# Expert weights of a mixture-of-experts decoder layer, loaded in 8 KB runs over permuted rows

## The chip, the cores and the metric

One core of a Trainium2 chip runs one decoder layer over 512 tokens of width 1024, in float32. The metric is device time in microseconds. The kernel before took 638.92 us, the median of 3 runs (637.88 to 639.37).

## What is computed

The layer is a mixer (gated linear attention and a gated convolution), then a hierarchical mixture of 16 experts, then a gated per-layer embedding and a last norm. The change touches the experts alone:

```
for e in range(N_EXPERTS):                      # 16; a token has 2 experts of its best group
    hid = silu(t @ w_gate[e]) * (t @ w_up[e])   # w_gate, w_up: 1024 x 512
    y = y + combine[:, e:e + 1] * (hid @ w_down[e])   # w_down: 512 x 1024
```

`t` is the normed residual stream. The order in which the rows of a weight matrix are summed over is free, as long as the columns of `t` or `hid` come in the same order.

## The kernel before

**Experts.** The normed tokens lie in DRAM as `h2d`, the residual stream as `xd`. For each expert, POOL gathers up to 96 tokens into `xe` (96 partitions x 1024, line 1056, in turn into two buffers, the gather for expert e+4 at the end of iteration e of the loop at line 1245, so a whole expert and more before its use). TensorE transposes them in eight blocks of 128 columns (`transposed`, line 1070, called by `x_tr`, line 1123, once for each half of the columns, four transposes each); ACT and DVE split each transposed block into two fp32r parts, `xT…h` and `xT…l`. `pu` and `pg` (96 x 512) are the products with w_up and w_gate, 24 matmuls each: 8 row blocks of the weights times 3 products of high and low parts (`mm3`, line 1094). silu(pg) * pu is `sg`; `h_tr` (line 1143) transposes it in four blocks to `hT`. `pd` is the product with w_down, in two column halves of 512, each 4 row blocks times 3 products, one half after the other (`stream_mm`, line 1101). ACT evicts each half with the tokens' weights to `ye` (lines 1264 and 1267), and POOL adds the rows of `ye` to `xd` in DRAM by a scatter (`scatter`, line 1112). In iteration e the order on TensorE is pu[e], pg[e+1], pd[e].

**The weights' stream.** `Stream` (line 54) holds a list of loads (`specs`) and a ring of slots of 128 partitions x 8 KB: 13 of them in the expert phase, two of which hold `prjs` (the product of the per-layer embeddings). Each load fills one slot with 1,024 KB. For gate and up it takes 512 rows of 512 columns, for down all 512 rows of 512 of the 1024 columns; row k*128 + p goes to partition p, so that a partition gets four runs of 2 KB (lines 94 to 98). A slot is taken apart in two halves: ACT casts a half (128 x 1024) to the tile `hi` (line 112), DVE computes the rest `lo` (line 113). A half is one `take()`: two row blocks of 512 columns, 6 matmuls. `pump()` starts the next half whenever fewer than `cap` are open (6, in the last four experts 5; `CAPS`). When its second half is done a slot goes back (`give`) and SP issues the next load of the list; `REST` holds back two freed slots in experts 8 to 11 and six from expert 12 on. The loads stand in the order in which TensorE needs them: up[e], gate[e+1], down[e], six for each expert (lines 742 to 750).

**Before and after the experts.** Ahead of expert 0, SP stores `xs` to `xd` and POOL gathers `xe` for experts 0 and 1 (line 1078) while SP issues three loads of experts; then a branch on the fullest expert's count (`overflow`, line 1146, line 1149) is passed; its body runs only where an expert has more than 96 tokens. After expert 14's scatter, SP reads `xd` back (`read_x`, line 1232) and loads w_ple_gate. Expert 15 is added by a matmul (line 1225) instead of a scatter.

Of the kernel before, what the change touches and what calls it, by code (L numbers as in the profile page):

```python
# [13 lines left out]
AF = mybir.ActivationFunctionType  # L14
# [4 lines left out]
P = 128  # L19
# [9 lines left out]
NE = 16  # L29
# [6 lines left out]
CAP = 96  # L36
CH = 2112
HALF = 512
# [14 lines left out]
class Stream:  # L53
# [11 lines left out]
    def add(self, src, r0, nk, c0, cn, c1=None, c1n=0, gain=None):  # L65
        self.specs.append((src, r0, nk, c0, cn, c1, c1n, gain))

    def slot(self, cols, dt=F32):

        at = self.free.pop(0)  # L70
        return at, at[0].tile([P, cols], dt, tag=at[1], name=at[1])
# [11 lines left out]
    def load(self, n=99, parts=1, eng=None):  # L83
        eng = eng or self.nc.sync
        while n and self.free and self.specs:
            n -= 1
            spec = self.specs.pop(0)
            if callable(spec):
                spec()
                continue  # L90
            src, r0, nk, c0, cn, c1, c1n, gain = spec
            w = cn + c1n
            at, raw = self.slot(nk * w)
            v = raw.rearrange("p (k c) -> p k c", k=nk)
            rows = src[r0:r0 + nk * P, :].rearrange("(k p) c -> p k c", p=P)
            for i in range(parts):
                ks = slice(nk // parts * i, nk // parts * (i + 1))
                eng.dma_start(v[:, ks, :cn], rows[:, ks, c0:c0 + cn])
                if c1n:
                    eng.dma_start(v[:, ks, cn:], rows[:, ks, c1:c1 + c1n])  # L100
            self.loaded += [(raw, nk // 2, w, 0, None, gain), (raw, nk // 2, w, 1, at, gain)]

    def split(self, hi=None, lo=None, eng=None, later=False):
        eng = eng or self.nc.vector
# [47 lines left out]
def hymba_layer(ctx, tc, x, p, g_mix, w_in, w_gla_gate, b_gla_gate, g_gla_out, w_conv, w_out,  # L152
# [4 lines left out]
    p, w_in, w_out = p[0, 0], w_in[0], w_out[0]  # L157
    ve, se, pe, ge, sy = nc.vector, nc.scalar, nc.tensor, nc.gpsimd, nc.sync
# [15 lines left out]
    def mm_ps(name):  # L174
        return ps.tile([P, HALF], F32, tag="mm", name=name)
# [4 lines left out]
    def half(i):  # L180
        return slice(i * HALF, (i + 1) * HALF)

    def tok(t):
        return slice(t * P, (t + 1) * P)


    W = Stream(nc, hlp, 6)

    def add_columns(src, c0, c1=None, c1n=0, gain=None):
        for i in range(2):  # L190
            W.add(src, HALF * i, 4, c0, HALF, c1, c1n, gain if gain is None else gain[:, 4 * i:4 * i + 4])
# [7 lines left out]
    ident = consts.tile([P, P], F32, name="ident")  # L199
# [515 lines left out]
    sgs = []  # L715
# [23 lines left out]

    W.specs += [lambda: read_p(), lambda: keep(pTt, F32R)]  # L740
    W.add(w_ple_proj[0], 0, 2, 0, D)
    add_columns(w_exp_gate[0, 0], 0)
    for e in range(NE):
        add_columns(w_exp_up[0, e], 0)
        if e == 0:
            W.specs += [lambda: keep(prjs, F32), lambda: keep(prjs, F32)]
        if e + 1 < NE:
            add_columns(w_exp_gate[0, e + 1], 0)
        for ci in range(2):
            W.add(w_exp_down[0, e], 0, 4, HALF * ci, HALF)  # L750
    sy.dma_start(xd[S:], x[:P])
    merged(proj_steps([f"pC{i}" for i in range(4)], c_out), gla[:12])
    merged(proj_steps([f"pu{i}" for i in range(4)], u_out), gla[12:])
# [150 lines left out]
    sw = rtp.tile([CAP, NE], F32, name="sw", bufs=1)  # L904
# [67 lines left out]
    for k in range(NK):  # L972
        if k % 2 == 0:
            wo.extend(W.take())
        wh, wl = wo[k]
# [9 lines left out]
    for t in range(NT):  # L985
        at = {1: lambda: (square0(t), x1_tr(t, 0))}
# [56 lines left out]
    ye = [mo.tile([P, D], F32, name=f"ye{i}") for i in range(2)]  # L1043
# [23 lines left out]
        return [(hh[:, k * n:(k + 1) * n], hl[:, k * n:(k + 1) * n]) for k in range(4)]  # L1067


    def transposed(src, name, n=CAP):  # L1070

        pt = aux_ps("pt_" + name)
        for k in range(4):
            pe.transpose(pt[:, k * n:(k + 1) * n], src[:n, tok(k)], ident[:n, :n])  # L1074
        return split_T(pt, name, n)

    for e in range(2):
# [16 lines left out]
    def mm3(dst, xT, ws, k0, nk):  # L1094
        for i, (wh, wl) in enumerate(ws):
            k = k0 + i
            xh, xl = xT[k]
            for n, (a, b_) in enumerate(((xh, wh), (xh, wl), (xl, wh))):
                pe.matmul(dst, a, b_, start=(k + n == 0), stop=(k == nk - 1 and n == 2))  # L1099

    def stream_mm(dst, xT, nk, then=(), ahead=True):

        then = dict(then)
        for h in range(nk // 2):
            mm3(dst, xT, W.take(), 2 * h, nk)
            W.done()
            if h in then:
                then[h]()
            if ahead:
                W.pump()  # L1110
# [6 lines left out]
    xTs, hTs, sgs, pgs, pus = {0: xT}, {}, {}, {}, {}  # L1117
# [5 lines left out]
    def x_tr(e, i):  # L1123
        if e < NE:
            xTs.setdefault(e, []).extend(transposed(xe[e % 2][:, half(i)], f"xT{e}_{i}"))
# [5 lines left out]
    def slots_mm(e):  # L1131
        if e < NE and e not in done:
            done.add(e)
            slots(e, oh[e], vals, toki, rowi, sw, f"{e}")

    def rows_of(e):
        if e < NE:
            gather(xe[e % 2][:CAP], col(toki, e))
# [2 lines left out]
        ve.tensor_mul(sgs[e][:CAP], sgs[e][:CAP], pus[e][:CAP])  # L1141

    def h_tr(e):
        hTs[e] = transposed(sgs[e], f"hT{e}")

    def overflow(free_x):

# [57 lines left out]
    def last_one_hot_tr():  # L1205
        pt = aux_ps("pt_ohl")
        for t in range(NT):
            pe.transpose(pt[:CAP, tok(t)], ohl[0][:, t * CAP:(t + 1) * CAP], ident)
        se.copy(ohT, pt[:CAP])
        a0, a1 = Af[:, :, NG - 1, EPG - 1], sec[:, :, NE - 1]  # L1210
        c0 = rt.tile([P, NT], F32, name="cwl0")
        ve.tensor_mul(c0, cw[0], a0)
        ve.tensor_mul(cwl, cw[1], a1)
        ve.tensor_add(cwl, cwl, c0)
# [30 lines left out]
    for e in range(NE - 1):  # L1245
        W.rest, W.cap = REST[e], CAPS[e]
        pus[e] = mm_ps(f"pu{e}")
        if e == 0:
            then = {0: lambda: (slots_mm(2), rows_of(2), slots_oh(3)), 1: lambda: x_tr(1, 0), 2: lambda: x_tr(1, 1),
                    3: lambda: (times_up(0), slots_mm(3), rows_of(3), slots_oh(4))}  # L1250
        else:
            then = {3: lambda: (times_up(e), slots_oh(e + 4))}
        stream_mm(pus[e][:CAP], xTs[e], NK, then)
        pgs[e + 1] = mm_ps(f"pg{e + 1}")
        then = {1: lambda: h_tr(e), 3: lambda: silu(e + 1)}
        if e == NE - 2:
            then[3] = lambda: (silu(e + 1), se.preload_act_table_set("sigmoid_and_others"))
        stream_mm(pgs[e + 1][:CAP], xTs[e + 1], NK, then)
        for ci in range(2):
            pd = mm_ps(f"pd{e}_{ci}")  # L1260
            y_ = ye[e % 2][:CAP, half(ci)]
            if ci == 0:
                first = last_one_hot if e == NE - 4 else lambda: slots_mm(e + 4)
                then = {0: first, 1: lambda: se.activation(y_, pd[:CAP], AF.Copy, scale=sw[:, e:e + 1])}
            else:
                then = {0: lambda: (x_tr(e + 2, 0), last_one_hot_tr() if e == NE - 4 else None),
                        1: lambda: (se.activation(y_, pd[:CAP], AF.Copy, scale=sw[:, e:e + 1]), x_tr(e + 2, 1), rows_of(e + 4))}  # L1267
            stream_mm(pd[:CAP], hTs[e], 4, then, ahead=(e < NE - 2 or ci == 0))
        scatter(ye[e % 2][:CAP], col(rowi, e))


    e = NE - 1
# [103 lines left out]
    for t in range(NT):  # L1376
        n = t + 1
# [78 lines left out]
```

## Time and profile before

| what | value |
|---|---|
| time, median of 3 runs | 638.92 us (637.88 to 639.37) |
| time of the profiled execution | 639.44 us |
| its span, first to last instruction | 637.7 us |
| mean granted TensorE clock | 0.982 of full speed |
| busy: TensorE, its weight loads, DVE, ACT, POOL | 94%, 72%, 75%, 57%, 19% of the span |
| read from and written to HBM | 137.56 MB, 12.71 MB |

The profile is of one execution. Its span leaves out 1.7 us at the two ends. An engine's busy share is a mean over stages: up to about 200 us the projections and the attention run, up to 260 us the output projection and the routing, up to about 575 us the experts, and then the gate of the embeddings. In the rows, L98 and so on are the lines of the kernel before; `raw` and `x` are slots of the stream, `xe`, `ye`, `pu`, `pg`, `pd`, `sg`, `hT` and `xT` the tiles named above, with buffer numbers left out.

### The profile page before, as it was taken

The page shows a single profiled execution, that of the slowest core. Times are in us where ns is not written, and L with a number is a line of the kernel's source. Part 1 is how long each engine was busy: PE and PEld are TensorE (multiplying, and loading weights), DVE is VectorE, ACT ScalarE, POOL GpSimd, SP SyncE. Part 2 cuts the span into 40 slices and gives each one's busy share as a digit, 9 for nine tenths or more (in the row PEclk, how much of TensorE's full clock was granted, in tenths as well). Part 3 has the DMA queues.
Part 4 walks back from the last instruction along what each step waited for, and adds up shares of the span by engine and source line. Part 5 has one row for each costly group of instructions (what it writes and reads, how often), then busy time and mean ns, then how long its engine had stood idle before and what let it go on. Part 6 is the DMA issues. An engine that isn't in the chain of part 4 may idle for free.

```text
span 637.7 us, 8404 instructions
## 1 busy us (share of the span) xinstructions
PE 601.3 (94%) x3006; PEld 457.7 (72%) x3006; DVE 478.1 (75%) x808; ACT 364.8 (57%) x516; POOL 119.9 (19%) x148
## 2 busy tenths in 40 slices
PE   7999989999999999559999999999999999988995
PEld 7987767877787787447777777777777767656784
DVE  4642897852496376457999999999999989888864
ACT  5433626203625233345788877778878878876332
POOL 1530842000240001103222211122222201100011
PEclk9999979999999999889999999999999999999999
DMA  8721211221034957884999999999999999987001
GB/s 270 236 68 67 99 67 66 67 67 66 1 132 154 389 163 286 294 304 150 333 369 368 367 352 353 355 347 348 350 367 360 357 340 361 370 261 277 33 34 66
DMA packets 73007, 148.45 MB, mean 233 GB/s; under 512 B 4797, under 2 KB 5396, under 8 KB 72942
## 3 DMA queue, kind: packets, MB, share of 16 engines
q1 hardware_dynamic: 69054, 136.69, 60.0%
q0 software_dynamic: 3744, 10.89, 7.6%
q8 instruction: 26, 0.43, 0.3%
q10 hardware_dynamic: 160, 0.27, 0.1%
q14 instruction: 23, 0.19, 0.1%
HBM read 137.56 MB, written 12.71 MB: 236 GB/s over the span
## 4 chain that ended last, share of the span: by engine, by line
PE 37%; DMA 9%; DVE 4%; ACT 3%; issue 2%; POOLq 0%; DVEq 0%; ACTq 0%
PE pu L1099 10%; PE pd L1099 10%; PE pg L1099 9%; DMA raw<-in_w_exp_down_dram 6%; PE pgate L1099 5%; DVE lo L113 2%; DMA x<-in_w_exp_down_dram 2%; ACT hi L112 2%; DMA x<-in_w_exp_up_dram 2%; PE pt_xT L1074 1%; PE pgate_last L1409 1%; DVE lo L118 1%; PE pt_hT L1074 1%; PE px L1306 1%; PE pz L1225 0%
## 5 line engine op out<-in xcount | busy, mean ns | idle before, releaser
L113 DVE TENSOR_TENSOR lo<-raw,hi 128x1024 fp32r<-128x1024 f32 x172 | 204.1, 1218 | 21.7 <-ACT hi L112 20.4
L112 ACT CAST hi<-raw 128x1024 fp32r<-128x1024 f32 x172 | 171.8, 1049 | 9.6 <-DMA raw<-in_w_exp_down_dram 8.2
L1056 POOL DMA_INDIRECT xe<-h2d,toki x16 | 28.1, 1759 | 199.9 <-PE pt_xT L1074 160.4
L118 DVE SCALAR_TENSOR_TENSOR lo<-raw,cst,hi 128x512 fp32r<-128x512 f32 (+1 forms) x52 | 41.4, 839 | 18.6 <-ACT hi L117 18.5
L113 DVE TENSOR_TENSOR lo<-x,hi 128x1024 fp32r<-128x1024 f32 x30 | 36.3, 1219 | 5.5 <-ACT hi L112 5.4
L1113 POOL DMA_INDIRECT xd<-ye,rowi x15 | 29.6, 1973 | 51.6 <-ACT ye L1267 47.9
L117 ACT ACTIVATE hi<-raw,cst 128x512 fp32r<-128x512 f32 (+1 forms) x52 | 34.0, 714 | 0.1
L112 ACT CAST hi<-x 128x1024 fp32r<-128x1024 f32 x30 | 30.9, 1050 | 1.7 <-DMA x<-in_w_exp_down_dram 1.4
L1099 PE MATMUL pg<-hi,xT_1h 128*96 128x512 f32 x60 | 24.5, 408 | 0.0
L1099 PE MATMUL pu<-hi,xT_0h 128*96 128x512 f32 x60 | 24.4, 407 | 0.0
L1099 PE MATMUL pu<-lo,xT_1h 128*96 128x512 f32 x60 | 23.8, 396 | 0.0
L1099 PE MATMUL pg<-hi,xT_1l 128*96 128x512 f32 x60 | 23.8, 396 | 0.0
L1099 PE MATMUL pu<-hi,xT_0l 128*96 128x512 f32 x60 | 23.8, 396 | 0.0
L1099 PE MATMUL pu<-hi,xT_1l 128*96 128x512 f32 x60 | 23.8, 396 | 0.0
L1099 PE MATMUL pg<-hi,xT_0h 128*96 128x512 f32 x60 | 23.7, 395 | 0.0
L1099 PE MATMUL pg<-lo,xT_1h 128*96 128x512 f32 x60 | 23.7, 395 | 0.0
L1099 PE MATMUL pg<-lo,xT_0h 128*96 128x512 f32 x60 | 23.7, 395 | 0.0
L1099 PE MATMUL pu<-lo,xT_0h 128*96 128x512 f32 x60 | 23.7, 395 | 0.0
L1099 PE MATMUL pg<-hi,xT_0l 128*96 128x512 f32 x60 | 23.7, 394 | 0.0
L1099 PE MATMUL pu<-hi,xT_1h 128*96 128x512 f32 x60 | 23.6, 394 | 0.0
L632 ACT ACTIVATE sq<-xs 128x512 f32<-128x512 f32 x4 | 2.5, 632 | 35.0 <-DVE xs L614 35.0
L724 POOL TENSOR_TENSOR xs<-xs,sg 128x128 f32<-128x128 f32 x16 | 11.3, 736 | 57.9 <-ACT sg L719 57.9
(539 smaller groups left out, 1591.1 us busy)
## 6 DMA issues: line engine op xcount, KB each, us to landing
raw<-in_w_exp_gate_dram SPq DMA_DIRECT2D x30, 1024.0 KB, 14.4
raw<-in_w_exp_down_dram SPq DMA_DIRECT2D x26, 1024.0 KB, 12.5
raw<-in_w_exp_up_dram SPq DMA_DIRECT2D x25, 1024.0 KB, 15.6
raw<-in_w_in_dram SPq DMA_DIRECT2D x10, 1024.0 KB, 5.1
x<-in_w_exp_up_dram SPq DMA_DIRECT2D x7, 1024.0 KB, 9.6
x<-in_w_exp_down_dram SPq DMA_DIRECT2D x6, 1024.0 KB, 17.5
xs<-in_x_dram SPq DMA_DIRECT2D x16, 256.0 KB, 5.5
raw<-in_w_out_dram SPq DMA_DIRECT2D x4, 1024.0 KB
```

The source lines that it names most:

```text
L112: self.nc.scalar.copy(hi, rw)
L113: los.append(lambda: eng.tensor_sub(lo, rw, hi.bitcast(F32)))
L117: self.nc.scalar.activation(hi[:, c_], rw[:, c_], AF.Copy, scale=g_)
L118: los.append(lambda c_=c_, g_=g_: eng.scalar_tensor_tensor(lo[:, c_], rw[:, c_], g_, hi[:, c_].bitcast(F32), op0=OP.mult, op1=OP.subtract))
L632: se.activation(osq[c], to[c], AF.Square)
L724: ge.tensor_tensor(tv, tv, sgs[i][:, tok(t)], op=OP.mult)
L1056: ge.indirect_dma_start(out=x_, out_offset=None, in_=h2d, in_offset=bass.IndirectOffsetOnAxis(ap=idx, axis=0), bounds_check=S - 1, oob_is_ ...
L1074: pe.transpose(pt[:, k * n:(k + 1) * n], src[:n, tok(k)], ident[:n, :n])
L1099: pe.matmul(dst, a, b_, start=(k + n == 0), stop=(k == nk - 1 and n == 2))
L1113: ge.indirect_dma_start(out=xd, out_offset=bass.IndirectOffsetOnAxis(ap=idx, axis=0), in_=y_, in_offset=None, bounds_check=S + P - 1, oob_ ...
L1306: pe.transpose(pt[:, tok(k)], X(t)[:, ci * HALF + k * P:ci * HALF + (k + 1) * P], ident)
L1409: pe.matmul(pgl[i][:, :256], a, b_[:, 256 * i:256 * i + 256], start=(k + n == 0), stop=(k == NK - 1 and n == 2))
```

## The change

`add_rows` adds a load of whole rows: of a block of nk*128 rows, partition p gets the nk consecutive rows p*nk to p*nk + nk - 1, one run of 8 KB in DRAM and in the slot. For gate and up nk is 4 (512 rows of 2 KB), for down nk is 2 (256 rows of 4 KB, all 1024 columns). Row block k of a slot is then every nk-th row instead of 128 consecutive ones. `transposed` follows: it reads the columns of `xe` with a step of 4 floats, those of `sg` with a step of 2. A half of a slot of down is now one row block of 1024 columns instead of two of 512, so both column halves, `pd[0]` and `pd[1]`, are summed side by side, and both are evicted after the last row block. Expert 15's down keeps the old form.

```diff
+    def add_rows(self, src, r0, nk):
+        self.specs.append((src, r0, nk, None, src.shape[-1], None, 0, None))
...
             at, raw = self.slot(nk * w)
+            self.loaded += [(raw, nk // 2, w, 0, None, gain), (raw, nk // 2, w, 1, at, gain)]
+            if c0 is None:
+                eng.dma_start(raw, src[r0:r0 + nk * P, :].rearrange("(p k) c -> p (k c)", k=nk))
+                continue
...
-    add_columns(w_exp_gate[0, 0], 0)
+    def add_expert(w):
+        for i in range(2):
+            W.add_rows(w, HALF * i, 4)
+
+    add_expert(w_exp_gate[0, 0])
     for e in range(NE):
-        add_columns(w_exp_up[0, e], 0)
+        add_expert(w_exp_up[0, e])
...
-        for ci in range(2):
-            W.add(w_exp_down[0, e], 0, 4, HALF * ci, HALF)
+        for i in range(2):
+            if e + 1 < NE:
+                W.add_rows(w_exp_down[0, e], 2 * P * i, 2)
+            else:
+                W.add(w_exp_down[0, e], 0, 4, HALF * i, HALF)
...
-    def transposed(src, name, n=CAP):
+    def transposed(src, name, n=CAP, nk=4):
         pt = aux_ps("pt_" + name)
         for k in range(4):
-            pe.transpose(pt[:, k * n:(k + 1) * n], src[:n, tok(k)], ident[:n, :n])
+            b_ = (k // nk) * nk * P
+            pe.transpose(pt[:, k * n:(k + 1) * n],
+                         src[:n, b_:b_ + nk * P].rearrange("n (p k) -> n k p", k=nk)[:, k % nk], ident[:n, :n])
...
     def h_tr(e):
-        hTs[e] = transposed(sgs[e], f"hT{e}")
+        hTs[e] = transposed(sgs[e], f"hT{e}", nk=2 if e + 1 < NE else 1)
...
-        for ci in range(2):
-            pd = mm_ps(f"pd{e}_{ci}")
-            y_ = ye[e % 2][:CAP, half(ci)]
...
-            stream_mm(pd[:CAP], hTs[e], 4, then, ahead=(e < NE - 2 or ci == 0))
+        pd = [mm_ps(f"pd{e}_{ci}") for ci in range(2)]
+        def y_out():
+            for ci in range(2):
+                se.activation(ye[e % 2][:CAP, half(ci)], pd[ci][:CAP], AF.Copy, scale=sw[:, e:e + 1])
+        then = {0: last_one_hot if e == NE - 4 else lambda: slots_mm(e + 4),
+                1: lambda: x_tr(e + 2, 0),
+                2: last_one_hot_tr if e == NE - 4 else nop,
+                3: lambda: (y_out(), x_tr(e + 2, 1), rows_of(e + 4))}
+        for k in range(4):
+            (wh, wl), = W.take()
+            for ci in range(2):
+                mm3(pd[ci][:CAP], [None] * k + [hTs[e][k]], [(wh[:, half(ci)], wl[:, half(ci)])], k, 4)
+            W.done()
+            then[k]()
+            if e < NE - 2 or k < 2:
+                W.pump()
```

On ACT, the rows around expert 14's down; ye is the eviction, hi the casts of the stream, hT the transposed sg. Before:

```order
L112 CAST hi<-x_5632 128x1024
L112 CAST hi<-raw_5674 128x1024
L1264 ACTIVATE ye_2307<-pd_0_5780,sw 96x512
L112 CAST hi<-raw_5674 128x1024
L1267 ACTIVATE ye_2307<-pd_1_5802,sw 96x512
L112 CAST hi<-raw_5700 128x1024 x2
```

and with the change:

```order
L120 CAST hi<-x_5641 128x1024
L120 CAST hi<-raw_5674 128x1024 x2
L1281 ACTIVATE ye_2307<-pd_0_5780,sw 96x512
L1281 ACTIVATE ye_2307<-pd_1_5781,sw 96x512
L120 CAST hi<-raw_5700 128x1024 x2
```

The eviction of pd_0 has moved behind the second cast of the slot, next to that of pd_1; the casts are the same.

On TensorE, the middle of expert 13's down with the first transposes of expert 15's xe. Before:

```order
L1099 MATMUL pd_0_5610<-hi,hT13h 96x512
L1099 MATMUL pd_0_5610<-lo,hT13h 96x512
L1099 MATMUL pd_0_5610<-hi,hT13l 96x512
L1099 MATMUL pd_1_5634<-hi,hT13h 96x512
L1099 MATMUL pd_1_5634<-lo,hT13h 96x512
L1099 MATMUL pd_1_5634<-hi,hT13l 96x512
L1099 MATMUL pd_1_5634<-hi,hT13h 96x512
L1099 MATMUL pd_1_5634<-lo,hT13h 96x512
L1099 MATMUL pd_1_5634<-hi,hT13l 96x512
L1074 MATMUL pt_xT_0_5641<-ident,xe_2306 128x96 x4
L1099 MATMUL pd_1_5634<-hi,hT13h 96x512
```

and with the change:

```order
L1117 MATMUL pd_0_5610<-hi,hT13h 96x512
L1117 MATMUL pd_0_5610<-lo,hT13h 96x512
L1117 MATMUL pd_0_5610<-hi,hT13l 96x512
L1117 MATMUL pd_1_5611<-hi,hT13h 96x512
L1117 MATMUL pd_1_5611<-lo,hT13h 96x512
L1117 MATMUL pd_1_5611<-hi,hT13l 96x512
L1091 MATMUL pt_xT_0_5628<-ident,xe_2306 128x96 x4
L1117 MATMUL pd_0_5610<-hi,hT13h 96x512
L1117 MATMUL pd_0_5610<-lo,hT13h 96x512
L1117 MATMUL pd_0_5610<-hi,hT13l 96x512
```

The two halves alternate, three matmuls each for a row block, and the transposes come after the second row block instead of after three quarters of the matmuls. The order of SP's loads and of POOL's instructions is the same as before.

## Rows read from the trace of the kernel before

**Rows 1.** The head of the page: the span, and busy time, share of the span and instructions of each engine; from its part on DMA, the queue on which SP issues the weights' loads, with its packets, MB and the share of 16 engines' time that they took.

```profile
span 637.7 us, 8404 instructions
...
PE 601.3 (94%) x3006; PEld 457.7 (72%) x3006; DVE 478.1 (75%) x808; ACT 364.8 (57%) x516; POOL 119.9 (19%) x148
...
q1 hardware_dynamic: 69054, 136.69, 60.0%
```

**Rows 2.** The table by stretches: the stretch (us from the span's start) and its length, then busy us and instructions of TensorE, its weight loads, DVE, ACT and POOL; then TensorE's granted clock, the DMA engines' share and GB/s. From 214 to 219 us only loads with 2 KB runs are under way; from 256 to 259 us the stores of xs to xd, and from 571 to 573 us the reads of xd, whose runs are 4 KB.

```profile
214.00:219.00 5.00, 5.00 (x25) 4.11 (x24) 2.76 (x4) 2.10 (x4) 0.00 (x0) 1.00 1.04 386
256.00:259.00 3.00, 2.57 (x25) 1.98 (x24) 2.41 (x17) 1.55 (x3) 0.00 (x0) 1.00 1.03 408
262.00:268.50 6.50, 0.28 (x2) 0.00 (x0) 0.51 (x1) 2.30 (x4) 0.22 (x1) 0.81 1.02 334
280.00:290.00 10.00, 3.27 (x13) 2.21 (x12) 2.53 (x9) 2.37 (x3) 0.00 (x0) 0.66 0.80 283
300.00:519.00 219.00, 219.00 (x1072) 155.32 (x1071) 204.03 (x288) 176.40 (x218) 45.40 (x25) 1.00 1.05 353
571.00:573.00 2.00, 2.00 (x10) 1.42 (x9) 2.00 (x3) 2.00 (x4) 0.00 (x0) 1.00 1.01 403
```

**Rows 3.** The chain of work that ended last, in order of time: start us, us, and what.

```profile
282.70 4.11 issue
...
323.39 0.33 PE pt_xT L1074 x4
...
325.45 5.59 PE pu L1099 x24
...
343.43 5.59 PE pu L1099 x24
...
500.13 17.63 DMA raw<-in_w_exp_down_dram
...
542.33 11.34 DMA x<-in_w_exp_down_dram
...
601.99 0.44 PE px L1306 x4
```

**Rows 4.** What TensorE waited for from 300 to 576 us: the engine, line and tile, whom it waited for, us in total, times, longest us.

```profile
PE pd L1099 <- DVE lo L113: 1.5, 3, 0.8
```

**Rows 5.** The timeline of TensorE: start us, us, engine, line, operation, out<-in, shape and count; in brackets the idle time before it and what ended it.

```profile
268.52 0.90 PE L1074 MATMUL pt_xT0a<-ident,xe 96*128 96x96 f32 x4 [6.24 <-DMA xe<-h2d,toki]
...
286.81 0.74 PE L1099 MATMUL pu<-hi,xT0ah 128*96 128x512 f32 x1 [6.73 <-issue]
...
519.28 0.40 PE L1099 MATMUL pd<-hi,hT12h 128*96 128x512 f32 x1
520.20 0.48 PE L1099 MATMUL pd<-lo,hT12h 128*96 128x512 f32 x1 [0.52 <-DVE lo L113]
...
557.70 0.47 PE L1099 MATMUL pd<-hi,hT14h 128*96 128x512 f32 x1
558.96 0.47 PE L1099 MATMUL pd<-lo,hT14h 128*96 128x512 f32 x1 [0.79 <-DVE lo L113]
```

**Rows 6.** What ACT waited for from 290 to 570 us; columns as in rows 4.

```profile
ACT hi L112 <- DMA raw<-in_w_exp_down_dram: 8.2, 6, 2.4
...
ACT hi L112 <- DMA x<-in_w_exp_down_dram: 1.4, 1, 1.4
```

**Rows 7.** The timeline of POOL, which issues the gathers (xe<-h2d) and scatters (xd<-ye); columns as in rows 5.

```profile
259.10 1.86 POOL L1056 DMA_INDIRECT xe<-h2d,toki  x1 [5.57 <-DVE cmaxi L931]
...
561.36 1.41 POOL L1113 DMA_INDIRECT xd<-ye,rowi  x1 [16.17 <-ACT ye L1267]
```

**Rows 8.** The timeline of SP's queue, which issues the loads; columns as in rows 5.

```profile
259.97 0.38 SPq L98 DMA_DIRECT2D raw<-in_w_exp_up_dram  x1
260.46 0.44 SPq L98 DMA_DIRECT2D x<-in_w_exp_up_dram  x1
261.01 0.45 SPq L98 DMA_DIRECT2D x<-in_w_exp_gate_dram  x1
...
569.01 0.82 SPq L1232 DMA_DIRECT2D raw<-xd  x2
```

**Rows 9.** All gathers, line 1056: the time from issue to landing.

```profile
DMA to landing us min/median/max: 5.2/8.1/9.4
```

**Rows 10.** The instructions on the tile pt_xT, the transposed xe: line, engine and operation, count, duration in ns (smallest, median, largest), first and last start, shapes.

```profile
L1074 PEld LDWEIGHTS pt_xT<-ident,xe x120: 137/138/143, 291.1 to 541.8; 96*128 96x128 f32 x120
L1074 PE MATMUL pt_xT<-ident,xe x120: 243/245/247, 291.3 to 541.9; 96*128 96x96 f32 x120
```

**Rows 11.** TensorE's weight loads by line and shape: count, busy us, mean ns, and the idle time before. The operand after the comma is the loaded one, partitions x columns.

```profile
L1099 PEld LDWEIGHTS pg<-lo,xT_1h 128*96 128x96 f32 x60 | 9.8, 163 | 3.2
...
L1225 PEld LDWEIGHTS pz<-raw,ohT 96*128 96x128 f32 x16 | 3.0, 188 | 0.8 <-DVE raw L1220 0.2
```

**Rows 12.** DVE's level products of the decayed keys (line 540); columns as in rows 10.

```profile
L540 DVE TENSOR_TENSOR xs<-F,qkT x28: 407/422/953, 74.5 to 116.8; 64x256 f32<-64x256 f32 x28
```

**Rows 13.** The timelines of ACT and of DVE around expert 14's eviction and the read of xd; columns as in rows 5.

```profile
560.40 0.69 ACT L1267 ACTIVATE ye<-pd,sw 96x512 f32<-96x512 f32 x1 [0.28 <-PE pd L1099]
...
574.94 0.75 DVE L1227 SCALAR_TENSOR_TENSOR raw<-pz,cwl,raw 128x512 f32<-128x512 f32 x1 [0.59 <-PE pz L1225]
```

**Rows 14.** The DMA issues: out<-in, engine, operation, count, KB each, median us from issue to landing.

```profile
raw<-xd SPq DMA_DIRECT2D x4, 512.0 KB, 4.4
```

More of the change, by code (lines that the diff above doesn't have):

```diff
@@ L100, in load @@
                     eng.dma_start(v[:, ks, cn:], rows[:, ks, c1:c1 + c1n])
-            self.loaded += [(raw, nk // 2, w, 0, None, gain), (raw, nk // 2, w, 1, at, gain)]
     def split(self, hi=None, lo=None, eng=None, later=False):
@@ L747, in hymba_layer @@
         if e + 1 < NE:
-            add_columns(w_exp_gate[0, e + 1], 0)
-        for ci in range(2):
-            W.add(w_exp_down[0, e], 0, 4, HALF * ci, HALF)
+            add_expert(w_exp_gate[0, e + 1])
+        for i in range(2):
[3 more added lines that the diff above has]
+                W.add(w_exp_down[0, e], 0, 4, HALF * i, HALF)
     sy.dma_start(xd[S:], x[:P])
@@ L1258, in hymba_layer @@
         stream_mm(pgs[e + 1][:CAP], xTs[e + 1], NK, then)
-        for ci in range(2):
-            pd = mm_ps(f"pd{e}_{ci}")
-            y_ = ye[e % 2][:CAP, half(ci)]
[L1262 to L1267, printed above, removed]
-            stream_mm(pd[:CAP], hTs[e], 4, then, ahead=(e < NE - 2 or ci == 0))
+        pd = [mm_ps(f"pd{e}_{ci}") for ci in range(2)]
[14 more added lines that the diff above has]
+                W.pump()
         scatter(ye[e % 2][:CAP], col(rowi, e))
```

## The prediction

> **What bounds the kernel now.** I read the page's head first: TensorE is busy for 601.3 of 637.7 us, and queue q1, which carries the weights, takes 60% of the DMA engines' time [rows 1]. So two things may bound it, and the share alone does not say which one does where. The second view is the table by stretches. From 300 to 519 us, twelve of the sixteen experts, TensorE is busy for 219.00 of 219.00 us, and the DMA share is 1.05 in the same rows [rows 2]. An expert takes 17.98 us there, the distance of two starts of pu [rows 3]. A faster DMA can therefore give nothing in this stretch: no TensorE time is idle to be taken back.
>
> The same rows show that the DMA is nevertheless short. An expert needs six loads of 1,024 KB, 6.29 MB, and 96 rows of 4 KB gathered and as many scattered, 0.39 MB each: 7.07 MB in 17.98 us, or 393 GB/s, while 353 GB/s arrive [rows 2, 3]. The difference, 0.7 MB an expert, comes out of the weights that already lie in the 11 slots left to the experts (two of the 13 hold prjs). After twelve experts that is 8.6 MB of 11.5, and from expert 8 on two of the slots, from 12 on six are held back as well. This is where the next views fit: the waits of TensorE between 300 and 576 us hold 1.5 us on DVE's lo parts of the weights, three times [rows 4]. The two that matter are at 519.28 and 557.70 us: the next matmul starts 0.92 and 1.26 us later, where 24 of them take 5.59 us, 0.23 us each [rows 3, 5]: 0.69 + 1.03 = **1.72 us lost**. Behind them is a load: ACT's casts waited for in_w_exp_down, and the chain shows 17.63 and 11.34 us between issue and landing [rows 3, 6]. 1.72 us is all that TensorE loses to weights in the expert phase, so it is the upper end of what faster loads can give there.
>
> Ahead of the expert phase are two other idle stretches in which the DMA plays a part. TensorE starts expert 0's transposes at 268.52 us after 6.24 us of waiting for the gather xe, issued at 259.10 us; three expert loads were issued between 259.97 and 261.01 us [rows 5, 7, 8]. And it idles 6.73 us up to 286.81 us, of which 4.11 us stand in the chain as issue, behind the branch on the fullest expert, with q1 at work (share 0.80, 283 GB/s) [rows 2, 3, 5].
>
> **The change, part by part.**
>
> *The loads.* 94 of the 96 expert loads get 8 KB runs instead of 2 KB; number, bytes, order and slots stay. 2 KB runs alone move 386 GB/s (214 to 219 us), transfers in 4 KB runs 403 to 408 GB/s (571 to 573 and 256 to 259 us), 4 to 6% more [rows 2]. No row has 8 KB runs into SBUF; I bound them by no gain and by twice the step from 2 to 4 KB, and take 5%, the middle of the rows. On the weights' part of the 353 GB/s, 314, that is some 16 GB/s: the shortage falls from 40 to 24 GB/s, 0.43 MB an expert or 5.2 MB after twelve, and the slots no longer run dry. I book **-1.72 us**; the other end is 0, if 8 KB go no faster. What is late next is nothing that loads decide: TensorE's own 17.98 us.
>
> *The gather of expert 0.* It shares the DMA engines with the three loads of 259.97 to 261.01 us, and at 9.4 us from issue to TensorE's start it matches the longest of the sixteen landings, the shortest being 5.2 us [rows 8, 9]. A gather of 96 rows puts 6 rows of 4 KB on each of the 16 engines. At 386 GB/s an engine moves 24.1 GB/s: a 2 KB run holds it for 0.085 us, an 8 KB run for 0.34 us. If each gathered row waits for one run of the load, six rows wait 6 x 0.25 = 1.5 us longer. Nothing hides it: TensorE has no other work at 262 us. The lower end is a gain of 0.4 us, 5% of the loads' 8.2 us, if they are out of the way earlier; the upper end is that the loads drain first: 3.15 MB at 386 GB/s from 261 us end at 269.2 us, 0.39 MB of rows take 1.0 us, and TensorE starts at 270.2 us, 1.6 us late. I take **+1.0 us**. The later gathers and scatters grow as well, but they have a whole expert, 17.98 us, before their rows are read.
>
> *The fetch behind the branch.* Its 4.11 us of issue fall into a stretch where q1 moves weights [rows 2, 3]. Nothing in the rows tells how many transfers it consists of; two that each wait for one run more make 2 x 0.25 = **+0.5 us**; ends 0 and 2 us, half of the 4.11 us again.
>
> *The transposes.* The weights' rows are permuted, so the 128 transposes of xe (32 groups of four) read every fourth column, 16 bytes apart, and 60 of sg every second; number and shapes stay. xe is the loaded operand: 138 ns for 128 columns [rows 10]. Four transposes take 0.33 us with 96 moving columns and 0.44 us with 128, both with 128 loaded ones [rows 3], so the pace is that of the moving side and the load lies beside it. No row shows a strided load. The nearest strided reads are DVE's level products, which take every second float at level 1 and runs of 64 at level 64: 407 ns the shortest, 422 ns the median of 28 [rows 12]. I book **0** and keep as bounds: nothing, and 50 ns for each of 128, the step from 138 ns to the 188 ns of the slower kind of load [rows 10, 11], 6.4 us. All of it would lie on the path, since TensorE has no idle time.
>
> *Down in one go.* Per expert the 24 matmuls, 4 casts and 4 lo parts are the same; pd0 and pd1 are both open from the start, from the same ring of four banks, which pu[e+1] and pg[e+2] don't touch. What moves is pd0's eviction: it now stands behind the last matmul, and the scatter comes one eviction, 0.69 us, later [rows 13]. For fourteen experts nobody waits for it. For expert 14, the scatter (POOL, 561.36 us) is waited for on SP's queue by the reads of xd (569.01 us), which land after 4.4 us, at 573.4 us, and DVE needs them at 574.94 us [rows 7, 8, 13, 14]: 1.5 us of cover, so 0. Without that cover, 0.7 us would show. The loads of w_ple_gate behind them on SP move with them and are used later still.
>
> *Sum.* -1.72 + 1.0 + 0.5 + 0 + 0 = -0.2 us against the profiled execution's 639.44 us. That execution is 0.52 us above the median of the three, 638.92 us, so the forecast is **638.7 us**: no change. From no change a measurement of this kernel can tell about 0.2%, 1.3 us.
>
> **The rivals.** *Faster (637.2 us).* Only the 1.72 us come off and neither gather nor fetch grows: 638.92 - 1.72. For it: the loads end earlier, and one gather in sixteen is all that is exposed. Against it: that gather runs in a stretch that is full, 334 GB/s at share 1.02 [rows 2].
>
> *Slower by the transposes (642.7 us).* The strided load becomes the pace of the transposes. It decides from 83 ns a load on, the pace of a group [rows 3]. Loads of the slower kind grow by 25 ns from 96 to 128 columns, 0.78 ns a column [rows 11], or 100 ns for 128: three of four in 32 groups then lose 17 ns (the first lies beside a long matmul), 1.6 us. At 50 ns for each it is 6.4 us; the middle is 4.0 us. For it: every transposed xe lies on a TensorE without idle time. Against it: the load has been beside the moving side so far. [...]
>
> [...]
>
> *Not what it says.* If 8 KB runs are cut into smaller pieces, rate, waits and gather stay as they are: 638.9 us. It counts with the forecast.
>
> **How the numbers follow.** Forecast 0.40, with 0.05 of it for runs cut in pieces; faster 0.26; slower by the transposes 0.22; slower at the start 0.12. Faster by over 0.2%: 0.26; within: 0.40; slower: 0.34. The range reaches from 636.8 us (all 1.72 us, and a little from the gather) to 643.4 us, past the middle of the transposes' case; its upper part and mishaps together stay out. The forecast's own range is 637.6 to 640.2 us.
>
> **What would show it.** Right: no wait on lo before 565 us, more GB/s from 300 to 519 us, the transposes still 0.33 us a group, an expert still 17.98 us, xe's first transposes up to 1.6 us later. [...] Wrong altogether: gains before 300 us, an expert faster than 17.98 us, or waits on lo that stay although the rate grew.

## The result, and the profile after

The changed kernel takes **641.98 us** (median of 6 runs, 640.66 to 642.75). The kernel before, measured beside it, takes 637.99 us (6 runs, 635.49 to 639.37). The ratio is 1.0061, with a 95% interval of 1.0039 to 1.0084: slower by 3.9 us, between 2.5 and 5.4. That is within the range given, but outside the forecast's own, and on the side of the case "slower by the transposes".

The profiled execution of the changed kernel took 641.09 us. Against the one of before (639.44 us) that is only 1.65 us more, because that one lay 1.45 us above the median of the 6 runs measured beside the changed kernel and this one 0.9 us below. So the size of the effect is read from the medians, and the profiles tell where it lies.

The head of the page and its line on the loads' queue; columns as in [rows 1]:

```profile
span 639.4 us, 8402 instructions
...
PE 603.1 (94%) x3006; PEld 463.6 (73%) x3006; DVE 480.3 (75%) x808; ACT 362.5 (57%) x516; POOL 118.2 (18%) x148
...
q1 hardware_dynamic: 32958, 136.69, 56.5%
```

The bytes on q1 are the same, in less than half as many packets: 8 KB runs are really made, and the DMA engines spend 56.5% of their time on them instead of 60.0% [rows 1]. TensorE's instructions are as many as before, and TensorE is busy for 1.8 us longer, its weight loads for 5.9 us. The table by stretches, columns as in [rows 2]:

```profile
214.00:219.00 5.00, 5.00 (x24) 3.79 (x23) 2.96 (x5) 2.95 (x5) 0.00 (x0) 1.00 1.01 419
262.00:268.50 6.50, 0.00 (x0) 0.00 (x0) 0.00 (x0) 1.49 (x2) 0.00 (x0) 0.74 1.01 353
300.00:519.00 219.00, 219.00 (x1057) 159.04 (x1056) 205.05 (x286) 173.17 (x217) 44.40 (x25) 1.00 1.00 367
```

Where loads run alone they move 419 GB/s instead of 386. From 300 to 519 us the rate rose by 14 GB/s only, since the share fell from 1.05 to 1.00 [rows 2]. What TensorE waited for from 300 to 576 us, columns as in [rows 4]:

```profile
PE pt_hT L1091 <- DVE sg L1159: 0.8, 1, 0.8
PE pd L1117 <- ACT hT15h L1080: 0.6, 1, 0.6
PE pd L1117 <- DVE lo L121: 0.2, 1, 0.2
```

The long waits on lo [rows 4, 5] are gone; one of 0.2 us is left. But TensorE did not finish earlier. The chain that ended last shows why, columns as in [rows 3]:

```profile
282.36 3.78 issue
...
303.63 0.44 PE pt_xT L1091 x4
...
306.85 0.44 PE pt_xT L1091 x4
307.29 5.59 PE pu L1117 x24
...
315.67 0.44 PE pt_hT L1091 x4
...
325.55 5.59 PE pu L1117 x24
```

**This is the line to read first.** Four transposes take 0.44 us instead of 0.33 [rows 3], those of xe (pt_xT) and those of sg (pt_hT) alike. Two starts of pu lie 18.26 us apart instead of 17.98. The tiles' instructions, columns as in [rows 10]:

```profile
L1091 PEld LDWEIGHTS pt_xT<-ident,xe x120: 196/210/222, 290.3 to 544.3; 96*128 96x128 f32 x120
L1091 PE MATMUL pt_xT<-ident,xe x120: 246/280/285, 290.6 to 544.4; 96*128 96x96 f32 x120
...
L1091 PEld LDWEIGHTS pt_hT<-ident,sg x64: 138/199/221, 297.0 to 568.8; 96*128 96x128 f32 x64
```

The load of 128 strided columns takes 210 ns instead of 138 [rows 10] for xe, 199 for sg, where the 138 ns are the four contiguous transposes of the last expert. On the mean 110 ns lie between two loads now (0.44 / 4), where the 96 moving columns set 83. The price does not fall on all four alike. The smallest matmul, 246 ns, is as before (243) and the others take some 280: the first transpose of a group, beside a long matmul, is not slowed. In the single records of the trace, matmuls within a group start 85, 115 and 122 ns apart and the next matmul follows after 67 ns; before, it was 85, 82, 81 and 28. So three of four lose some 37 ns each.

Expert 0's first eight transposes pay nothing. Their loads, before and with the change, and the stretch in which they run with the change:

```profile
L1074 PEld LDWEIGHTS pt_xT0a<-ident,xe x4: 183/228/231, 268.5 to 268.9; 96*128 96x128 f32 x4
```

```profile
L1091 PEld LDWEIGHTS pt_xT0a<-ident,xe x4: 197/222/226, 268.6 to 269.0; 96*128 96x128 f32 x4
```

```profile
268.00:270.50 2.50, 1.90 (x10) 1.80 (x11) 0.43 (x1) 0.78 (x2) 0.00 (x0) 0.50 1.02 315
```

The granted clock is 0.50 there, in both kernels. The contiguous load takes 228 ns instead of 138, the strided one 222 instead of 210, and four transposes take 0.92 us where the contiguous ones took 0.90 [rows 5]. The timelines of TensorE and POOL at the start of expert 0, columns as in [rows 5, 7]:

```profile
268.60 0.92 PE L1091 MATMUL pt_xT0a<-ident,xe 96*128 96x96 f32 x4 [7.15 <-DMA xe<-h2d,toki]
```

```profile
258.28 1.86 POOL L1071 DMA_INDIRECT xe<-h2d,toki  x1 [5.59 <-DVE cmaxi L946]
```

From the gather's issue to TensorE 10.32 us pass; before, it was 9.42 [rows 5, 7].

### The profile page after: what moved, and what is told of

Its sections match the earlier page's. It is cut to its first block, busy times and chain, and to the rows that moved or that the text cites. A ratio compares the mean times of both kernels' runs of the same rounds, so it can differ in the third digit from the quotient of the medians.

```text
span 639.4 us, 8402 instructions
## 1 busy us (share of the span) xinstructions
PE 603.1 (94%) x3006; PEld 463.6 (73%) x3006; DVE 480.3 (75%) x808; ACT 362.5 (57%) x516; POOL 118.2 (18%) x148
## 3 DMA queue, kind: packets, MB, share of 16 engines
q1 hardware_dynamic: 32958, 136.69, 56.5%
## 4 chain that ended last, share of the span: by engine, by line
PE 52%; DVE 2%; issue 1%; ACT 1%; POOLq 0%; DVEq 0%; ACTq 0%
PE pu L1117 14%; PE pd L1117 14%; PE pg L1117 13%; PE pgate L1117 5%; PE pt_xT L1091 2%; PE pt_hT L1091 1%; PE pgate_last L1435 1%; DVE lo L126 1%; PE px L1332 1%; PE pz L1243 0%; DVE raw L1245 0%; ACT hi L120 0%; PE pslot L928 0%; DVE lo L121 0%; ACT hi L125 0%
## 5 line engine op out<-in xcount | busy, mean ns | idle before, releaser
L1071 POOL DMA_INDIRECT xe<-h2d,toki x16 | 22.8, 1423 | 204.2 <-PE pt_xT L1091 164.3
L1131 POOL DMA_INDIRECT xd<-ye,rowi x15 | 33.3, 2221 | 51.4 <-ACT ye L1281 47.8
```

The costliest lines, as they stand in the source:

```text
L1071: ge.indirect_dma_start(out=x_, out_offset=None, in_=h2d, in_offset=bass.IndirectOffsetOnAxis(ap=idx, axis=0), bounds_check=S - 1, oob_is_ ...
L1131: ge.indirect_dma_start(out=xd, out_offset=bass.IndirectOffsetOnAxis(ap=idx, axis=0), in_=y_, in_offset=None, bounds_check=S + P - 1, oob_ ...
```

## The experiments

Ten kernels, each timed in turn with the kernel before on the same chip. **Theory A:** a step over columns makes TensorE's weight load the pace of a transpose, for xe and sg alike; all else is worth little. **Rival B:** the longer runs disturb SBUF or the engines, and the transposes are longer for that.

**r1: the strided transposes alone, loads as before.**

```diff
-            pe.transpose(pt[:, k * n:(k + 1) * n], src[:n, tok(k)], ident[:n, :n])
+            b_ = (k // nk) * nk * P
+            pe.transpose(pt[:, k * n:(k + 1) * n],
+                         src[:n, b_:b_ + nk * P].rearrange("n (p k) -> n k p", k=nk)[:, k % nk], ident[:n, :n])
...
-        hTs[e] = transposed(sgs[e], f"hT{e}")
+        hTs[e] = transposed(sgs[e], f"hT{e}", nk=2 if e + 1 < NE else 1)
```

> The kernel before, with one part of the change alone: the transposes read every fourth column of xe and every second of sg; every load stays as it was, so the products pair other rows of the weights with the tokens' columns, with the same number of operations and bytes. Theory A (a strided load on TensorE sets the pace of a transpose): a group of four takes 0.44 to 0.45 us for xe and for sg instead of 0.33, an expert about 18.3 us instead of 17.98; 15 experts x 0.3 = 4.5 us, less the 1.72 us of waits on lo, which shrink as TensorE needs the weights later: +3 to +4.5 us on the kernel before, 641 to 642.5 us. Rival B (the longer groups of the changed kernel come from the longer runs that the DMA writes into SBUF at the same time): groups 0.33 us, expert 17.98 us, the time of the kernel before.

Measured: 641.53 us (12 runs) against 638.35 (26 runs), ratio 1.0043 [1.0026, 1.0060]. The chain of r1:

```profile
307.35 0.44 PE pt_xT L1075 x4
307.79 5.59 PE pu L1101 x24
...
316.17 0.44 PE pt_hT L1075 x4
...
326.09 5.59 PE pu L1101 x24
```

The table by stretches of r1, and what TensorE waited for on lo from 300 to 576 us:

```profile
300.00:519.00 219.00, 219.00 (x1055) 158.80 (x1054) 204.35 (x286) 174.88 (x216) 44.08 (x25) 1.00 1.04 354
```

```profile
PE pd L1101 <- DVE lo L113: 0.2, 1, 0.2
```

The strided read alone gives 0.44 us a group, 18.30 us an expert and the time of the changed kernel. Rival B falls. Note the second half: the waits on lo are gone here too, with 2 KB runs and 354 GB/s. A TensorE that needs 0.32 us longer an expert gives the loads that time. "No wait on lo" is therefore no proof that loads became faster, and beside the longer transposes the faster loads had nothing left to save.

**r2: the loads alone, contiguous transposes.**

```diff
-                         src[:n, b_:b_ + nk * P].rearrange("n (p k) -> n k p", k=nk)[:, k % nk], ident[:n, :n])
+                         src[:n, tok(k)], ident[:n, :n])
```

> The changed kernel with contiguous transposes (the tokens' columns are not permuted, so the products pair other rows; operations and bytes are the same). Theory A: a group takes 0.33 us, an expert 17.95 to 18.0 us, no wait on lo before 565 us, the gather of expert 0 still about 10.3 us from issue to TensorE's start: 5 us below the changed kernel, about 637 us, which is 1 to 1.7 us below the kernel before. Rival B (longer runs slow the transposes): groups 0.44 us and the changed kernel's time, 642 us.

Measured: 636.90 us (8 runs), ratio 0.9970 [0.9957, 0.9984]. The chain and the table by stretches of r2:

```profile
307.44 0.33 PE pt_xT L1091 x4
307.77 5.59 PE pu L1117 x24
...
316.15 0.33 PE pt_hT L1091 x4
...
325.70 5.59 PE pu L1117 x24
```

```profile
300.00:519.00 219.00, 219.00 (x1074) 155.72 (x1073) 206.93 (x289) 176.70 (x221) 46.51 (x25) 1.00 1.00 367
```

Groups are back at 0.33 us, with the long runs and 367 GB/s; the wait on lo is 0.2 us. The loads, with down in one go, make the kernel faster by 1.9 us (1.0 to 2.7). An expert takes 17.93 us, a little less than before.

**r4: gate and up as in the change, down as before** (2 KB runs, two halves in turn, sg contiguous). **r7** is r4 with contiguous transposes of xe as well.

```diff
-        for i in range(2):
-            if e + 1 < NE:
-                W.add_rows(w_exp_down[0, e], 2 * P * i, 2)
-            else:
-                W.add(w_exp_down[0, e], 0, 4, HALF * i, HALF)
+        for ci in range(2):
+            W.add(w_exp_down[0, e], 0, 4, HALF * ci, HALF)
...
-        hTs[e] = transposed(sgs[e], f"hT{e}", nk=2 if e + 1 < NE else 1)
+        hTs[e] = transposed(sgs[e], f"hT{e}", nk=1)
```

> The changed kernel with down as before: 2 KB runs, two column halves one after the other, sg's transposes contiguous; gate and up keep 8 KB runs and xe's strided transposes. Theory A: only xe's eight groups... two of three groups an expert are strided: groups of xe 0.44 us, of sg 0.33 us, an expert 17.98 + 0.22 = 18.2 us, no long wait on lo; 15 x 0.11 = 1.6 us below the changed kernel, about 640.3 us. Rival D (down's order in one go is what makes the expert longer): expert 17.98 us and about 638 us. Rival E (sg's step of two is free): the changed kernel's expert of 18.26 us.

> The kernel with gate and up in 8 KB runs and down as before (r4), with contiguous transposes (tokens' columns not permuted, the products pair other rows; operations and bytes are the same). It tells down's order apart: against the loads alone (r2) only down differs. Theory H (down in one go shortens an expert by 0.04 to 0.05 us, as pd's 24 matmuls do, 5.63 instead of 5.67 us): groups 0.33 us, an expert 17.97 us where r2 has 17.93, no long wait on lo: 0.7 us above r2, 637.5 us. Rival: down's order is free, 17.93 us and r2's time; or down's 2 KB runs bring the waits on lo back, up to 1.7 us: 638.5 us.

Measured: r4 641.59 us (7 runs), 1.0040 [1.0025, 1.0056]; r7 638.07 us (11 runs), 0.9989 [0.9978, 1.0000]. The chain of r4:

```profile
308.32 0.44 PE pt_xT L1088 x4
308.77 5.59 PE pu L1114 x24
...
317.14 0.33 PE pt_hT L1088 x4
...
326.96 5.59 PE pu L1114 x24
```

xe's groups 0.44, sg's 0.33: rival E falls, sg's step of two was not free. The expert takes 18.19 us, as theory A said; rival D falls. r4's time is 1.3 us above what was expected, which had left out that **down in one go** is worth something: an expert takes 17.98 us in r7 and 17.93 in r2, 15 x 0.05 = 0.75 us, which r4 gives up. That is 0.75 of the 1.3 us. r2 and r7 differ in down's order and in its runs (8 KB and 2 KB); which of the two shortens the expert was not tried apart. The chain of r7, and what its TensorE waited for on lo:

```profile
308.23 0.33 PE pt_xT L1088 x4
308.56 5.59 PE pu L1114 x24
...
326.54 5.59 PE pu L1114 x24
```

```profile
PE pd L1114 <- DVE lo L121: 0.2, 1, 0.2
```

The long waits on lo stay away in both, so gate's and up's runs are enough for that. r7 is the cleanest row on the loads: TensorE keeps the 17.98 us of the kernel before, and the long waits are gone all the same.

**r3: the writer permutes.** h2 is written in permuted order by DVE's product of the norm, and sg x pu likewise; TensorE reads contiguous columns.

```diff
-            ve.scalar_tensor_tensor(h2[t][i], X(t)[:, half(i)], rs_moe[t], gmoe[:, half(i)],
-                                    op0=OP.mult, op1=OP.mult)
+            rows4 = lambda z: z.rearrange("n (p k) -> n k p", k=4)
+            ve.scalar_tensor_tensor(h2[t][i].rearrange("n (k p) -> n k p", k=4), rows4(X(t)[:, half(i)]), rs_moe[t],
+                                    rows4(gmoe[:, half(i)]), op0=OP.mult, op1=OP.mult)
...
+        rows2 = lambda z: z[:CAP].rearrange("n (b p k) -> n b k p", b=2, k=2)
+        ve.tensor_mul(sgs[e][:CAP].rearrange("n (b k p) -> n b k p", b=2, k=2), rows2(sg), rows2(pus[e]))
```

> The changed kernel's loads, but the permutation is made by the instruction that writes the rows: DVE's last product of the norm reads every fourth column and writes h2 in permuted order, and DVE's product of sg and pu reads every second column; TensorE's transposes read contiguous columns. Theory A: as with the loads alone, 0.33 us a group and 17.95 to 18.0 us an expert, about 637 us, and DVE's two products are no longer than before by more than 0.1 us each. Rival C (a stride costs DVE what it cost TensorE): the product of sg and pu, between the end of pu and the transposes of sg, grows by half or more, but sg's transposes come later than pd of the expert before, so it is hidden; the norm's products stand ahead of the first gather and would show there, by up to 1 us: 638 us.

Measured: 637.58 us (12 runs), 0.9983 [0.9969, 0.9997]. DVE's two products, grouped by line (busy us, mean ns), in the kernel before and in r3:

```profile
L1141 DVE TENSOR_TENSOR sg<-sg,pu 96x512 f32<-96x512 f32 x16 | 10.8, 676 | 1.7 <-PE pu L1099 1.7
...
L858 DVE SCALAR_TENSOR_TENSOR h<-xs,rsmoe,gmoe 128x512 f32<-128x512 f32 x8 | 5.6, 746 | 0.4 <-POOL rsmoe L854 0.4
```

```profile
L1165 DVE TENSOR_TENSOR sp<-sg,pu 96x512 f32<-96x512 f32 x15 | 10.1, 676 | 0.0
...
L874 DVE SCALAR_TENSOR_TENSOR h<-xs,rsmoe,gmoe 128x512 f32<-128x512 f32 x8 | 8.8, 1140 | 0.4 <-POOL rsmoe L869 0.4
```

In these two instructions on DVE a step of two is free (676 ns both) and a step of four costs 0.39 us on 746; no run gives one instruction both steps. The last tile pays the 0.39 us twice ahead of the router, 0.8 us. r3's median lies 0.7 us above r2's, which fits, but the two intervals overlap. Rival C is right for the norm, wrong for sg.

**r5 and r6: the gather first.** r5 is r3, r6 is the kernel before, each with the three expert loads near 260 us held back on SP's queue by a small copy that reads xe.

```diff
+    load_, W.load = W.load, lambda *a, **k: None
     lo1()
...
+    landed = mo.tile([P, 4], F32, name="landed")
+    sy.dma_start(landed[:CAP], xe[0][:CAP, :4])
+    W.load = load_
     W.free += [(ring, f"x{i}") for i in range(2)]
     W.load()
```

> The kernel whose writers permute (r3), with the three expert loads of 259 to 260 us held back on SP's queue until the gather of expert 0 has landed. Theory F (the gather is slow because it shares the DMA engines with those loads, and longer runs hold it longer): from issue to TensorE's first transposes 5 to 6.5 us, the shortest landings of the other gathers, instead of 10; TensorE starts expert 0 some 4 us earlier; the loads end where the DMA stood nearly idle before (271 to 276 us, 69 GB/s), so no wait on lo appears: about 633.5 us, 4 us below r3. Rival G (the gather's time is its own): 9 to 10 us as before, and nothing is gained, or up to 1 us lost: 637.5 to 638.5 us.

> The kernel before (2 KB runs), with the same three loads held back until the gather of expert 0 has landed. Theory F: the gather then takes the same 5 to 6.5 us as in r5, whatever the runs' length, and the difference of 0.9 us between 2 KB and 8 KB runs vanishes with it; TensorE starts expert 0 some 3 us earlier, the waits on lo near 519 and 557 us stay or grow by up to 1.7 us as TensorE asks for weights earlier: 634.5 to 636.5 us. Rival G: 9.4 us from issue to TensorE, as before, and 638.4 us.

Measured: r5 **631.05 us** (6 runs) against 638.41 (17 runs), 0.9872 [0.9851, 0.9894]; r6 634.52 us (6 runs), 0.9943 [0.9929, 0.9957]. TensorE's timeline in r5, and in r6:

```profile
263.90 0.55 PE L1093 MATMUL pt_xT0a<-ident,xe 96*128 96x96 f32 x4 [1.87 <-DMA xe<-h2d,toki]
```

```profile
263.34 0.55 PE L1075 MATMUL pt_xT0a<-ident,xe 96*128 96x96 f32 x4 [1.76 <-DMA xe<-h2d,toki]
```

The gathers were issued at 258.86 and 258.40 us: 5.04 and 4.94 us to TensorE, with 8 KB and with 2 KB runs. Theory F holds, rival G falls: more than four of the gather's 9.4 us [rows 5, 7] are the three loads. With them out of the way, it no longer matters how long their runs are. Where the loads run beside the gather, it took 9.3 to 9.5 us with 2 KB runs (before, r1, r8, r10) and 10.2 to 10.4 with 8 KB runs (after, r2, r3, r4, r7): 0.9 us apart, each group within 0.2.

r6 came out at the lower end of what was expected, r5 came 2.4 us below what was expected. r5's trace shows where part of that lies. The gather gives 5.1 us against r3 (10.16 us there), where 4 were booked. An expert is 0.05 us shorter than in r3 (r10, below). And TensorE, idle for 1.87 us ahead of the first transposes instead of r3's 6.98, runs them faster: four take 0.55 us instead of 0.90. The granted clock from 262 to 268.5 us is 0.74 in r5 and 0.69 in r3, and in r3 it is 0.50 from 265 to 271 us.

**r8: longer steps**, r1 with xe read every eighth column and sg every fourth.

```diff
-            b_ = (k // nk) * nk * P
+            b_ = 0
...
-                         src[:n, b_:b_ + nk * P].rearrange("n (p k) -> n k p", k=nk)[:, k % nk], ident[:n, :n])
+                         src[:n, b_:b_ + nk * P].rearrange("n (p k) -> n k p", k=nk)[:, k0 + k], ident[:n, :n])
...
-            xTs.setdefault(e, []).extend(transposed(xe[e % 2][:, half(i)], f"xT{e}_{i}"))
+            xTs.setdefault(e, []).extend(transposed(xe[e % 2], f"xT{e}_{i}", nk=8, k0=4 * i))
```

> The transposes alone (r1, loads as before), with longer steps: xe read every eighth column instead of every fourth, sg every fourth instead of every second; the products pair other rows, operations and bytes are the same. Theory A1 (any step over one element costs a load the same): groups 0.44 us as in r1, an expert 18.3 us and 641.5 us. Rival A2 (the price grows with the step): groups of xe 0.55 us or more, an expert 18.5 us or more, 645 us or more.

Measured: 641.49 us (5 runs) against 638.34 (18 runs), 1.0037 [1.0018, 1.0056]. The chain of r8:

```profile
308.04 0.41 PE pt_xT L1075 x4
308.45 5.58 PE pu L1101 x24
...
316.82 0.44 PE pt_hT L1075 x4
```

A step of eight costs no more than r1's step of two (0.41 and 0.44 us a group): within the steps tried, from two to eight, any step has a price, and it does not grow. A1 holds.

**r9: the gain permuted once**, r5 with gmoe permuted ahead by GpSimd, so that DVE's norm has one strided operand.

```diff
-                                    rows4(gmoe[:, half(i)]), op0=OP.mult, op1=OP.mult)
+                                    gmoe[:, half(i)].rearrange("n (k p) -> n k p", k=4), op0=OP.mult, op1=OP.mult)
...
+    for i in range(2):
+        ge.tensor_copy(h2[0][i], gmoe[:, half(i)])
+        ge.tensor_copy(gmoe[:, half(i)].rearrange("n (k p) -> n k p", k=4), h2[0][i].rearrange("n (p k) -> n k p", k=4))
```

> The kernel whose writers permute and that gathers first (r5), with the norm's gain permuted once beforehand by GpSimd, so that DVE's product reads only one strided operand. In r3 and r5 that product takes 1.14 us instead of 0.75, twice for the last tile, ahead of the router's path to the first gather. Theory J (each strided operand adds its half): 0.95 us, 0.4 us earlier at the gather, 630.6 us. Rival K (one strided operand is free, the second costs): 0.75 us, 0.8 us earlier, 630.2 us. Rival L (one strided operand costs all of it): 1.14 us and 631.0 us.

Measured: 630.65 us (5 runs), 0.9872 [0.9854, 0.9890], the same ratio as r5. DVE's product in r9:

```profile
L874 DVE SCALAR_TENSOR_TENSOR h<-xs,rsmoe,gmoe 128x512 f32<-128x512 f32 x8 | 8.7, 1131 | 0.4 <-POOL rsmoe L869 0.4
```

1,131 ns: one operand with a step of four costs DVE all of it. That is rival L, and nothing is gained. The time alone would have fitted theory J's 630.6 us; the row decides.

**r10: a spare tile.** In r5 and r6 an expert was 0.05 to 0.08 us shorter than in r3 and before, which the gather does not explain.

```diff
+    spare = mo.tile([P, 4], F32, name="spare")
+    ve.memset(spare, 0.0)
```

> The kernel before with nothing but a spare tile of 16 bytes a partition behind xe and ye in SBUF, which is set once and not read; it shifts every tile allocated after it. In r5 and r6, which have such a tile, 24 matmuls of pu take 5.55 to 5.56 us instead of 5.59 and an expert 17.88 to 17.90 us where 17.93 to 17.98 was expected. Theory M (the shifted place of the tiles in SBUF does it): an expert 17.90 us, 15 x 0.08 = 1.2 us below the kernel before, 637.2 us. Rival N (the delayed loads do it): 17.98 us and 638.4 us.

Measured: 638.99 us (12 runs), 1.0007 [0.9990, 1.0023]. The chain of r10, and what TensorE waited for on lo; then the first and last of the same rows before:

```profile
307.97 5.55 PE pu L1101 x24
...
325.87 5.55 PE pu L1101 x24
...
560.16 5.78 PE pu L1101 x24
```

```profile
PE pd L1101 <- DVE lo L113: 1.3, 3, 0.8
```

```profile
307.48 5.59 PE pu L1099 x24
...
560.36 5.77 PE pu L1099 x24
```

Of the expert theory M is right: 17.90 us with nothing but tiles shifted by 16 bytes. Of the time it is not borne out: 637.2 us were expected. From the first pu of these chains to the last, r10 takes 252.19 us and the kernel before 252.88, so 0.7 us of gain stand in the profile; the time, 0.4 us above that of before (-0.6 to +1.5), shows none. The long waits on lo stay (1.3 us, before 1.5 [rows 4]), so they are not what ate it; where it went is open. Why the shifted place is faster was not tried.

## Why the prediction was wrong

**The step that failed** is the one on the transposes: "so the pace is that of the moving side and the load lies beside it", "I book 0". Measured, with r1's 18.30 us an expert: 0.32 us for three groups, 0.107 us each, times 45 groups (30 of xe, 15 of sg; the two of expert 0, at a granted clock of 0.50, take 0.92 and 0.84 us against 0.90 and 0.85) = **+4.8 us**. The 0.33 and 0.44 us of [rows 3] did show that the moving side set the pace of contiguous loads; they said nothing of a strided one. A load of 138 ns at a pace of 83 already overlaps with its neighbours, and how near it is to setting the pace can't be read from such rows. With no row for the strided load, the case deserved more than 0.22 beside 0.40 for a price of 0.

The rival named the mechanism. An expert grows by twelve times the growth of a transpose, xe's eight and sg's four: 12 x 27 ns on the mean = 0.32 us. The rival also had right that the first of four is spared. Two parts of its sum were too small: its lower price was 17 ns on three of four transposes where some 37 ns fell on each of the three, and it left sg's 15 groups out. Its upper price, 50 ns on every transpose, was too large, so its middle of 4.0 us came near the 4.8 for the wrong reasons. A step of two does not spare TensorE's weight load: a group of sg takes 0.44 us with it (r1) and 0.33 without (r4). On DVE the product of sg and pu takes 676 ns with a step of two and without, the norm's product 1,140 ns with a step of four instead of 746 (r3).

**The loads, -1.72 us: right, and then worthless.** r7 and r2 show them: no long waits, in r7 at the same 17.98 us an expert as before. r2 is 1.9 us faster, with the small gain of down; r7 alone, 0.7 us (0 to 1.4), hardly tells itself from no change. But 8 KB runs alone ran at 419 GB/s, 8.5% above the 386 [rows 2], not 5%. Beside the longer transposes the term is not the loads' any more: r1 has no long waits either.

**The gather, +1.0 us: right.** 10.32 - 9.42 = 0.9 us, and the other kernels fall into the same two groups. The size is partly luck: the working by runs gave 1.5 us, and 1.0 was picked from the range without a reason. That the loads drain first, the upper end, did not happen: TensorE started 10.32 us after the issue, not 11.1. That each gathered row waits for one run of a load was the author's estimate; the traces show the 0.9 us and not what it consists of.

**The fetch, +0.5 us: wrong in size, 0.** No run shows that this piece of issue consists of transfers that wait for runs of the loads; from 281 to 287 us the two instruction queues moved one packet each, before the change and with it. The piece of issue is 3.78 us after the change; with 2 KB runs it is 4.11 (before), 3.75 (r1) and 3.71 (r6), with 8 KB runs 3.31 (r3) to 3.82 (r5). It varies by more than the run length moves it. So the slower start, 0.12 of the chances, did not come beyond the gather's 0.9 us.

**Down in one go, 0: nearly.** Together with down's 8 KB runs it gains 0.05 us an expert, 0.75 us (r7 against r2). The later scatter cost nothing. DVE's first product on what was read from xd, columns as in [rows 13]:

```profile
576.60 0.75 DVE L1245 SCALAR_TENSOR_TENSOR raw<-pz,cwl,raw 128x512 f32<-128x512 f32 x1 [0.60 <-PE pz L1243]
```

It waits for TensorE's pz, as before, and not for the read.

The terms together, in us against the kernel before. The gain of down is left out where down is as before, and the waits on lo are counted as gone wherever they are:

| kernel | transposes | waits on lo | gather | down | norm | sum | measured (interval) |
|---|---|---|---|---|---|---|---|
| after | +4.8 | -1.7 | +0.9 | -0.75 | 0 | +3.2 | +3.9 (2.5 to 5.4) |
| r1 | +4.8 | -1.7 | 0 | 0 | 0 | +3.1 | +2.7 (1.7 to 3.8) |
| r2 | 0 | -1.7 | +0.9 | -0.75 | 0 | -1.6 | -1.9 (-2.7 to -1.0) |
| r3 | 0 | -1.7 | +0.9 | -0.75 | +0.8 | -0.8 | -1.1 (-2.0 to -0.2) |
| r4 | +3.2 | -1.7 | +0.9 | 0 | 0 | +2.4 | +2.6 (1.6 to 3.6) |
| r7 | 0 | -1.7 | +0.9 | 0 | 0 | -0.8 | -0.7 (-1.4 to 0.0) |

Every sum of the table lies within its interval, so nothing as large as the transposes is missing. Terms below some 0.7 us are shown by the traces alone, not by these times.

## What to carry to other kernels

A permutation that costs the DMA nothing (419 GB/s with it and 8 KB runs, 386 without) is paid where it is undone (four transposes in 0.44 us instead of 0.33): on an engine without idle time a price that no row shows is not zero, and it is multiplied by all instructions that it touches. Let an engine with slack, or one that reads the step in the same time (DVE's product of sg and pu, 676 ns both ways, r3), write the permuted order, and count a wait as saved only if nothing else in the same change fills its place. Look at the exposed wait first: holding back three loads until one gather of 0.39 MB had landed gave more (r6, 0.57%, with the shifted tiles that alone, in r10, gave no time) than the faster loads (r2, 0.30%, with down in one go), and together with the writer's permutation it made the fastest kernels here, r5 and r9, 1.3% below before.

## What was not expected of the hardware

- TensorE's load of 128 columns takes 138 ns contiguous and, with the change, 199 with a step of two and 210 with a step of four; four transposes then take 0.44 us instead of 0.33. A step of eight (0.41 us, r8) is no worse. At a granted clock of 0.50 the contiguous load takes 228 ns and the strided one 222, and four transposes take 0.90 and 0.92 us.
- DVE's product of sg and pu is as long with a step of two as without (676 ns, r3); in the norm's product one operand with a step of four is as slow as two (1,131 ns in r9 and 1,140 in r3, against 746).
- 16 bytes of shift in SBUF shortened 24 matmuls from 5.59 to 5.55 us (r10). Why stays open.
- Loads of 1,024 KB in 8 KB runs moved 419 GB/s, in 2 KB runs 386.
